# The order of the contraction tiles inside a weight block: even ones and odd ones together

## The chip, the cores and the metric

The kernel runs on one core of a Trainium2 chip. The metric is the device time of one execution in microseconds (us). The engines are TensorE (PE in the profile; its weight loads are listed apart as PEld), VectorE (DVE), ScalarE (ACT), GpSimd (POOL) and the engine that issues most transfers (SP).

## The reference

One layer of a hybrid decoder is computed for 256 positions of a new sequence and 8 × 4 positions of sequences that are under way, 288 rows of width 2048 in all, in float32:

```python
proj = x @ w_in
gB, gC, h, q, k, v, z, b_logit, a_logit, m_a, m_b = jnp.split(proj, split_points, axis=-1)
conv_out, new_conv_a = causal_depthwise_conv(gC * h, conv_a_buf, conv_a_w)
y_a = (gB * conv_out) @ w_a_out
...
o, S = gated_delta_rule(qh, kh, vh, g, beta, S0.astype(jnp.float32))
...
y_b = o.reshape(Bsz, L, D_GDN).astype(x.dtype) @ w_b_out
merged = jax.nn.sigmoid(m_a) * y_a + jax.nn.sigmoid(m_b) * y_b
x = layer_norm(ALPHA * x + merged @ w_o, ln1_g, ln1_b)
hid = jnp.square(jax.nn.relu(x @ w_up))
x = layer_norm(ALPHA * x + hid @ w_down, ln2_g, ln2_b)
```

Nearly all the work is in the products with the six large matrices: `w_in` (2048 × 11280), `w_a_out` and `w_b_out` (1024 × 2048), `w_o` (2048 × 2048), `w_up` (2048 × 8192) and `w_down` (8192 × 2048).

## The kernel before

**Products.** Activations lie transposed, the contraction on the partitions in tiles of 128, and the 288 rows along the free dimension. A product is made as out.T: the weights are the operand that is loaded into TensorE (128 × 128 at a time), the activations the one that streams past (128 × 288). To keep float32 accuracy each operand is split into a high part, rounded to a shorter format, and a low part, the rest. Three of the four products are made: high × high, high × low and low × high.

**Blocks.** The weights are read in blocks of 512 KB: 4 tiles of the contraction by 256 columns (`KB = 4`, `GW = 256`). The list `blocks`, filled by `add_group` (L154), holds all of them in the order of work. A group is a run of blocks that sum into one pair of PSUM banks, one bank for each 128 columns: 4 blocks where the contraction is 2048 long, 2 where it is 1024. There are 496 blocks: 176 of `w_in` and, between its last 64, 16 of `w_a_out` and 16 of `w_b_out`; then 32 of `w_o`; then four rounds of 32 of `w_up` and 32 of `w_down`. Blocks 0 to 47 are the groups of k, q and v. The first four blocks are wider (2 tiles by 512 columns) and serve two groups at once. The last four, marked `by_token`, are multiplied in another function with the operands exchanged.

**Stages of a block.** The main loop (L1667) goes over the block numbers `i`. SP loads the block into a `raw` tile (`load`, L191). ScalarE casts it to the high part (`split_hi`, L207, the instruction at L212); VectorE subtracts the high part from the raw block for the low part (`split_lo`, L214; it goes through the helper `tt`, so its instruction is listed at L143). From block 10 on both are done for block `i + 3` while block `i` is multiplied. A block's two parts lie in one of four buffers, `wbuf[i % 4]` (L163). Each buffer has two halves 1056 numbers (4224 bytes) apart: the even tiles of the block, high and low, are in one and the odd tiles in the other; two tiles of one half lie 256 numbers (1024 bytes) apart (`weight_halves`, L167). In a wide block a half holds one tile with its 512 columns.

**The matmuls of a block.** `matmuls(i)` (L221) goes over the tiles `k` of the block, and for each makes six matmuls. For each of the two column halves, the high weights meet the high and then the low activations (four matmuls, L245); then the low weights of each column half meet the high activations (two, L247). Every matmul has a weight load of its own. A block is 24 matmuls. `st` marks the tile whose first matmul starts a new sum in the bank, and `en` the tile whose last matmul ends it. After the last block of a group its evacuation (the functions in `gi["evac"]`) runs during the next blocks.

**What sets the order.** The program's order is written out by hand (`tc.manual_schedule()`): every engine executes its instructions in the order in which the program issues them. Waits between engines are put in from the tiles that they write and read: a matmul waits for the cast or the subtraction that wrote its weights and for the instruction that wrote its activations, and a cast into a buffer waits for the last matmul that read that buffer's high part. Between blocks the loop issues other work: the evacuations that are due, and up to the merge phase one step of the delta rule (`sgen`) for a block, with small matmuls of its own on TensorE.

Of the kernel before, what the change touches and what calls it, by code (L numbers as in the profile page):

```python
# [106 lines left out]
def hybrid_kernel(ctx: ExitStack, tc: tile.TileContext, A):  # L107
# [15 lines left out]
    def nm(s):  # L123
        counter[0] += 1
        return f"{s}{counter[0]}"
# [61 lines left out]
    def at(i, f):  # L187
        due.setdefault(i, []).append(f)
# [32 lines left out]
    def matmuls(i):  # L221
        gi, r0, k0, first, last = blocks[i]
        if gi.get("by_token"):
            return first_tokens(i, k0)
        members = gi.get("pair", (gi,))
        if first:
            for m in members:
                m["ps"] = acp.tile([P, 2, 512], F32, tag="acc", name=nm("acc"))
        ps = members[0]["ps"]
        h, l = his.pop(i), los.pop(i)  # L230
        ah, al = gi["acts"]()
        n = gi["width"]
        kb = gi["kb"]
        h, l = ([u[:, k % 2, k // 2] for k in range(KB)] if kb == KB else
                [u[:, k].rearrange("p u c -> p (u c)") for k in range(2)] for u in (h, l))
        for k in range(kb):
            xh_, xl_ = ah[:, k0 + k, 0:n], al[:, k0 + k, 0:n]
            st = first and k == 0
            en = last and k == kb - 1
            per = gi["cols"] // P // len(members)  # L240
            for u, m in enumerate(members):
                ts = [(m["ps"][:, t, 0:n], slice((per * u + t) * P, (per * u + t + 1) * P)) for t in range(per)]
                both = [(o, c, x) for o, c in ts for x in (xh_, xl_)]
                for o, c, x in both[::2] + both[1::2] if i == 0 else both:
                    pe.matmul(o, h[k][:, c], x, start=st and x is xh_, stop=False)  # L245
                for o, c in ts:
                    pe.matmul(o, l[k][:, c], xh_, start=False, stop=en)  # L247
                    if fill:
                        fill.pop(0)()
        if last:  # L250
            for n, f in enumerate(gi["evac"]):
                at(i + 1 + n, lambda f=f: f(ps))
# [514 lines left out]
    def first_tokens(i, k0):  # L767
        kept.append((his.pop(i), los.pop(i)))
        a = ph["acc"]
        if k0 == 0:  # L770
            ph["T0"] = acp.tile([P, 2, 512], F32, tag="acc", name=nm("acc"))[:, 0]
            for k in range(2):
                pe.matmul(ph["T0"][:, 256 + k * P:256 + k * P + P], a[:, 14 + k, 0:P], ident,
                          start=k == 0, stop=False, is_transpose=True)
            sample_copy(0)
            sample_copy(1)
            ph["sg2"] = gtile()
            sample_turn(2, True)
            pe.matmul(ph["sg2"][:, 256:512], cst("sel96"), ph["s4"], start=False, stop=True)
        products(ph["T0"][:, 256:512], 0, k0 // KB)  # L780
# [886 lines left out]
    for i in range(len(blocks)):  # L1667
# [72 lines left out]
        if i == mark["end"] - 1:  # L1740
            sample_products()
        matmuls(i)
        if i == 4:
            x_last()
# [47 lines left out]
```

## Time and profile before

| | us |
|---|---|
| median of 3 runs | 1642.29 (1642.19 to 1642.38) |
| the profiled execution, its own time | 1642.29 |
| its span, first to last instruction | 1640.2 |
| VectorE busy | 981.1 |
| ScalarE busy | 785.4 |
| VectorE's subtraction of 128 × 1024 at L143 (mean of 493) | 1.225 |
| ScalarE's cast of 128 × 1024 at L212 (mean of 493) | 1.048 |

How to read the profile: "busy" is the time in which an engine had an instruction under way. TensorE's matmuls overlap, so the mean duration of one (some 0.29 us) is longer than the distance between the starts of two; its pace is read from starts, or from the number of matmuls in a stretch. In a view by time a row gives the start in us from the start of the span, the duration, the engine, the line and the operands, and a row with "x2" stands for two instructions that overlap. In a view by windows a row gives the start and end of a stretch, its length, and for each engine its busy time and, in brackets, the number of instructions. The rows of waits give the waiting engine and line, what it waited for, the total, the number of times and the longest.

### The profile page before, as it was taken

To read this page: it belongs to the slowest core of one execution; us is meant where nothing else is said; L and a number is where in the kernel's file an instruction comes from. 1 tells how busy PE (TensorE), PEld (TensorE's weight loads), DVE (VectorE), ACT (ScalarE), POOL (GpSimd) and SP (SyncE) were. 2 spreads that over 40 slices of the span, in tenths; PEclk is the share of its full clock that TensorE was granted. 3 is DMA by queue.
4 is the path that set the end of the run, shared out by engine and by line. 5 is a ranking of instruction groups with operands and counts; after the bars stand their busy time and mean duration, and the time that the engine had idled before them with its cause. 6 is when DMAs were issued, how large, how long until landed. Compare 5 with 4: busy or idle time off the path is not lost.

```text
span 1640.2 us, 31402 instructions
## 1 busy us (share of the span) xinstructions
PE 1631.2 (99%) x13130; PEld 1616.4 (99%) x13130; DVE 981.1 (60%) x1299; ACT 785.4 (48%) x1231; POOL 139.0 (8%) x273
## 2 busy tenths in 40 slices
PE   9999999999999999999999999999999999999998
PEld 8999999999999999999999999999999999999998
DVE  6798688767544444457776666554444444444566
ACT  6786756448533333434444445443334433344454
POOL 1142216133000000000000000000000000000111
PEclk9999999999999999999999999999999999999999
DMA  8655457645655555555565555555555555555653
GB/s 265 184 175 168 142 174 202 182 127 171 200 167 168 168 167 168 168 168 166 166 221 159 164 169 165 169 169 168 168 167 168 168 169 168 168 167 169 182 165 102
DMA packets 273236, 280.42 MB, mean 171 GB/s; under 512 B 13727, under 2 KB 267220, under 8 KB 272832
## 3 DMA queue, kind: packets, MB, share of 16 engines
q1 hardware_dynamic: 269190, 266.06, 53.7%
q0 software_dynamic: 3616, 12.02, 2.4%
q8 instruction: 103, 1.69, 0.4%
q14 instruction: 39, 0.32, 0.1%
q10 hardware_dynamic: 288, 0.33, 0.1%
HBM read 270.88 MB, written 7.48 MB: 170 GB/s over the span
## 4 chain that ended last, share of the span: by engine, by line
PE 99%; DMA 0%; DVE 0%; ACT 0%; SPq 0%; issue 0%
PE acc L245 63%; PE acc L247 31%; PE acc L765 1%; DMA raw<-in_w_in_dram 0%; PE g L1351 0%; PE g L1523 0%; PE g L1543 0%; PE g L1546 0%; PE g L1342 0%; PE g L1243 0%; PE g L1501 0%; PE g L1535 0%; PE g L1057 0%; PE g L982 0%; PE g L719 0%; PE g L1418 0%
## 5 line engine op out<-in xcount | busy, mean ns | idle before, releaser
L143 DVE TENSOR_TENSOR w<-raw,w 128x1024 fp32r<-128x1024 f32 (+1 forms) x503 | 607.3, 1210 | 561.3 <-ACT w L212 559.6
L212 ACT CAST w<-raw 128x1024 fp32r<-128x1024 f32 (+1 forms) x499 | 518.2, 1041 | 711.3 <-PE acc L245 643.2
L245 PE MATMUL acc<-xh,w 128*128 128x288 f32 x1408 | 396.4, 298 | 0.7 <-ACT w L1625 0.4
L245 PE MATMUL acc<-xl,w 128*128 128x288 f32 x1408 | 390.8, 293 | 0.1
L247 PE MATMUL acc<-xh,w 128*128 128x288 f32 x1408 | 299.2, 293 | 0.5 <-DVE w L143 0.5
L245 PE MATMUL acc<-dh,w 128*128 128x288 f32 (+1 forms) x1024 | 287.1, 296 | 0.0
L245 PE MATMUL acc<-dl,w 128*128 128x288 f32 (+1 forms) x1024 | 285.6, 294 | 0.0
L245 PE MATMUL acc<-hh,w 128*128 128x288 f32 x992 | 276.9, 295 | 0.0
L245 PE MATMUL acc<-hl,w 128*128 128x288 f32 x992 | 275.3, 293 | 0.0
L245 PEld LDWEIGHTS acc<-xh,w 128*128 128x128 f32 x1408 | 264.4, 188 | 3.7 <-issue 1.6
L245 PEld LDWEIGHTS acc<-xl,w 128*128 128x128 f32 x1408 | 264.2, 188 | 1.2 <-DVE xl L143 0.3
L247 PEld LDWEIGHTS acc<-xh,w 128*128 128x128 f32 x1408 | 224.4, 188 | 1.0 <-DVE w L143 0.9
L247 PE MATMUL acc<-dh,w 128*128 128x288 f32 (+1 forms) x1024 | 217.3, 293 | 0.0
L247 PE MATMUL acc<-hh,w 128*128 128x288 f32 x992 | 209.6, 292 | 0.0
L245 PEld LDWEIGHTS acc<-dh,w 128*128 128x128 f32 x1024 | 192.4, 188 | 0.0
L245 PEld LDWEIGHTS acc<-dl,w 128*128 128x128 f32 x1024 | 192.3, 188 | 0.0
L245 PEld LDWEIGHTS acc<-hh,w 128*128 128x128 f32 x992 | 186.4, 188 | 0.4 <-issue 0.4
L245 PEld LDWEIGHTS acc<-hl,w 128*128 128x128 f32 x992 | 186.2, 188 | 0.0
L247 PEld LDWEIGHTS acc<-dh,w 128*128 128x128 f32 x1024 | 163.4, 188 | 0.0
L247 PEld LDWEIGHTS acc<-hh,w 128*128 128x128 f32 x992 | 157.7, 188 | 0.0
L245 PE MATMUL acc<-mh,w 128*128 128x288 f32 x256 | 71.4, 295 | 0.0
L245 PE MATMUL acc<-ml,w 128*128 128x288 f32 x256 | 71.0, 293 | 0.0
(420 smaller groups left out, 1477.3 us busy)
## 6 DMA issues: line engine op xcount, KB each, us to landing
raw<-in_w_in_dram SPq DMA_DIRECT2D x175, 512.0 KB, 3.8
raw<-in_w_up_dram SPq DMA_DIRECT2D x128, 512.0 KB, 3.6
raw<-in_w_down_dram SPq DMA_DIRECT2D x128, 512.0 KB, 3.6
raw<-in_w_o_dram SPq DMA_DIRECT2D x32, 512.0 KB, 4.3
raw<-in_w_a_out_dram SPq DMA_DIRECT2D x16, 512.0 KB, 3.6
raw<-in_w_b_out_dram SPq DMA_DIRECT2D x16, 512.0 KB, 3.6
S<-in_state_gdn_dram POOLq DMA_DIRECT2D x8, 512.0 KB, 5.1
out_dram<-S POOLq DMA_DIRECT2D x8, 512.0 KB, 4.1
```

The lines of the kernel that those rows point to most:

```text
L143: dve.tensor_tensor(out=out, in0=a, in1=b, op=op)
L212: act.copy(his[i][:, a, b], r[:, a, b])
L245: pe.matmul(o, h[k][:, c], x, start=st and x is xh_, stop=False)
L247: pe.matmul(o, l[k][:, c], xh_, start=False, stop=en)
L765: pe.matmul(out, x[:, kk, c], w[:, k % 2, k // 2], start=False, stop=stop)
```

## The change

In the inner loop of `matmuls`, the tiles of a block are no longer taken as 0, 1, 2, 3. From block 10 on, odd-numbered blocks take 0, 2, 1, 3 and even-numbered ones 1, 3, 0, 2. The marks for the start and the end of a sum go with the first and the last tile of the new order. Blocks 0 to 9 keep the old order, and the last four blocks, which leave `matmuls` earlier, are not touched. The number of matmuls and their operands are the same.

```diff
@@ -233,10 +233,11 @@
         kb = gi["kb"]
         h, l = ([u[:, k % 2, k // 2] for k in range(KB)] if kb == KB else
                 [u[:, k].rearrange("p u c -> p (u c)") for k in range(2)] for u in (h, l))
-        for k in range(kb):
+        ks = ((0, 2, 1, 3) if i % 2 else (1, 3, 0, 2)) if i > 9 else range(kb)
+        for k in ks:
             xh_, xl_ = ah[:, k0 + k, 0:n], al[:, k0 + k, 0:n]
-            st = first and k == 0
-            en = last and k == kb - 1
+            st = first and k == ks[0]
+            en = last and k == ks[-1]
             per = gi["cols"] // P // len(members)
             for u, m in enumerate(members):
```

## The prediction

> **What bounds the kernel now.** I looked first at the clock and the span, then at the share of each engine, then at the chain that ended last, then at TensorE's own waits.
>
> ```profile
> span 1640.2 us, 31402 instructions
> PE 1631.2 (99%) x13130; PEld 1616.4 (99%) x13130; DVE 981.1 (60%) x1299; ACT 785.4 (48%) x1231; POOL 139.0 (8%) x273
> ...
> PE 99%; DMA 0%; DVE 0%; ACT 0%; SPq 0%; issue 0%
> PE acc L245 63%; PE acc L247 31%; PE acc L765 1%; DMA raw<-in_w_in_dram 0%; PE g L1351 0%; PE g L1523 0%; PE g L1543 0%; PE g L1546 0%; PE g L1342 0%; PE g L1243 0%; PE g L1501 0%; PE g L1535 0%; PE g L1057 0%; PE g L982 0%; PE g L719 0%; PE g L1418 0%
> ...
> PE acc L247 <- DVE w L143: 0.5, 1, 0.5
> PE acc L245 <- ACT w L1625: 0.4, 1, 0.4
> ```
>
> TensorE is busy for 99% of the span, and 94% of the chain are the two lines that the change reorders, L245 and L247. These matmuls wait for another engine only in single cases of half a microsecond. So the time is the number of matmuls times their pace; nothing else matters unless it makes TensorE wait. The pace comes from a view by windows:
>
> ```profile
> core 0: us, PE busy (x) PEld busy (x) DVE busy (x) ACT busy (x) POOL busy (x), PEclk, DMA share, GB/s
> 430.00:710.00 280.00, 280.00 (x2138) 280.00 (x2137) 132.14 (x120) 109.22 (x115) 0.00 (x0) 1.00 0.58 167
> 1330.00:1610.00 280.00, 280.00 (x2138) 280.00 (x2137) 142.13 (x151) 112.07 (x138) 9.33 (x27) 1.00 0.56 170
> ```
>
> Both stretches hold 2138 matmuls in 280 us at full granted clock (PEclk 1.00): 280 / 2138 = 131 ns each. The reader should see what differs between them: other activation tiles at other places, another matrix, 10 us more of VectorE work, GpSimd at work in one only. The count is the same to one in 2138, or 0.05%. The pace thus comes from the kind and order of the instructions (each with its own weight load), not from what the other engines write meanwhile.
>
> **The change part by part.**
>
> *Instructions.* None is added or removed. Each tile of the contraction still takes six matmuls of the same shapes, and a block its 24; the number of weight loads, casts, subtractions and transfers stays as it is. This part costs 0.
>
> *How many blocks.* The change acts from block 10 on and not in the last four blocks, which take another path.
>
> ```profile
> raw<-in_w_in_dram SPq DMA_DIRECT2D x175, 512.0 KB, 3.8
> raw<-in_w_up_dram SPq DMA_DIRECT2D x128, 512.0 KB, 3.6
> raw<-in_w_down_dram SPq DMA_DIRECT2D x128, 512.0 KB, 3.6
> raw<-in_w_o_dram SPq DMA_DIRECT2D x32, 512.0 KB, 4.3
> raw<-in_w_a_out_dram SPq DMA_DIRECT2D x16, 512.0 KB, 3.6
> raw<-in_w_b_out_dram SPq DMA_DIRECT2D x16, 512.0 KB, 3.6
> ```
>
> One such transfer brings one block: 495, and with the first block, which comes in pieces, 496. Less 10 and less 4 leaves 482 blocks. The even tiles of a block lie in one half of its weight buffer and the odd ones in the other. The old order 0, 1, 2, 3 changes the half at each of four tile changes (the one into the next block included). The new order (0, 2, 1, 3 in odd blocks; 1, 3, 0, 2 in even ones) changes it only in the middle of a block, because a block starts in the half in which the last one ended. So 3 × 482 = 1446 tile changes that now cross from one half to the other will stay in one half.
>
> *What a tile change inside one half costs.* From block 10 on the trace of before has none, but block 2 does. There the columns are twice as wide, one half holds one tile with all 512 columns, and the twelve matmuls of a tile go to two groups, six and six. A step from the first six to the second stays in the half, and makes the same jump in the buffer as a step from tile 0 to 2 or 1 to 3 does in the new order. Starts, in the view by time:
>
> ```profile
> 15.58 0.30 PE L245 MATMUL acc<-xh,w 128*128 128x288 f32 x1
> ...
> 17.15 0.29 PE L245 MATMUL acc<-xh,w 128*128 128x288 f32 x1
> ...
> 17.94 0.29 PE L245 MATMUL acc<-xh,w 128*128 128x288 f32 x1
> ...
> 18.73 0.30 PE L245 MATMUL acc<-xh,w 128*128 128x288 f32 x1
> ```
>
> The six that end with a step inside the half (17.15 to 17.94) take 0.79 us, and the six that end with a crossing (17.94 to 18.73) take 0.79 us as well. The whole of block 2, with two crossings, takes 18.73 - 15.58 = 3.15 us. An ordinary block with four:
>
> ```profile
> 22.89 0.30 PE L245 MATMUL acc<-xh,w 128*128 128x288 f32 x1
> ...
> 26.03 0.30 PE L245 MATMUL acc<-xh,w 128*128 128x288 f32 x1
> ```
>
> takes 3.14 us. Two crossings less made no difference beyond the 0.01 us to which the view gives a start. I take 0 ns for a tile change inside a half against one that crosses; the ends that the resolution leaves are 0.01 us over two crossings, 5 ns either way. Another reason for 0: five of the six loads of any tile already follow a load from the same half, so the new order brings no new kind of neighbour. What block 2 can't show is the other operand, whose tile stays there and changes by two in the new order; but the matmuls of a tile already take turns between two activation tiles that lie much farther apart. Sum: 1446 × 0 = 0, with ends at 1446 × 5 ns = 7.2 us either way.
>
> *The release of a weight buffer.* ScalarE may cast block i+3 into a buffer when the last matmul with the high parts of block i-1 has read it; VectorE then fills the low parts.
>
> ```profile
> ACT w L212 <- PE acc L245: 643.2, 344, 4.0
> ...
> 999.25 1.05 ACT L212 CAST w<-raw 128x1024 fp32r<-128x1024 f32 x1 [0.25 <-PE acc L245]
> ...
> 1000.33 1.23 DVE L143 TENSOR_TENSOR w<-raw,w 128x1024 fp32r<-128x1024 f32 x1 [1.49 <-ACT w L212]
> ```
>
> The last matmul of that kind is the 22nd of its block, whichever tile comes last, so the cast starts when it does now. Even a shift of a whole tile, 0.79 us, would be covered: the low parts are ready at 1000.33 + 1.23 = 1001.56, and their block starts three blocks after 999.3, at about 1008.7, 7 us later. The queues of ScalarE, VectorE, SP and POOL keep their order, and no wait is added in any. Cost 0. Without that cover it would be as in this place of the chain in order of time, where a subtraction came late and the one wait of 0.5 us above arose:
>
> ```profile
> 122.05 1.23 DVE w L143
> ```
>
> *A tile taken earlier than now.* The third or fourth tile of a block may now come second or first, and its activations must be there by then. The tightest place is a last pair of tiles that the preceding group has just produced.
>
> ```profile
> 1130.48 0.75 DVE L143 TENSOR_TENSOR hl<-r,hh 128x576 fp32r<-128x576 f32 x1
> ...
> 1134.62 0.29 PE L245 MATMUL acc<-hh,w 128*128 128x288 f32 x1
> ```
>
> This pair is complete at 1130.48 + 0.75 = 1131.23, and the block that reads it starts at 1134.62. Even read first in its block it would have been there for 3.4 us. Cost 0. The first matmul of a group (which starts the accumulation) and the last keep their places, so the evacuation of each sum starts as before.
>
> **Sum.** 0 + 0 + 0 + 0 on a profiled execution of 1642.29 us (span 1640.2, some 2 us around it), which is also the median of the runs shown (1642.29, from 1642.19 to 1642.38). I predict **1642.3 us**. Two kernels count as different here from 0.2% on, 3.3 us.
>
> **The rivals.**
>
> *A, slower: a jump inside a half delays TensorE.* Two tiles of one half lie 1024 bytes apart; a load right behind one from the same half but another tile could take longer. The pace does depend on the form of the operands:
>
> ```profile
> 825.00:915.00 90.00, 90.00 (x669) 90.00 (x668) 60.62 (x72) 42.46 (x62) 0.00 (x0) 1.00 0.57 182
> 925.00:1015.00 90.00, 90.00 (x688) 90.00 (x688) 63.17 (x76) 46.46 (x60) 0.00 (x0) 1.00 0.55 167
> ```
>
> With 290 columns in place of 288 (the first row) a matmul takes 90 / 669 = 134.5 ns against 90 / 688 = 130.8: two columns of 288 should bring 0.9 ns and brought 3.7. If each jump cost that, 1446 × 3.7 = 5.4 us: 1647.7. It counts from 3.3 / 1446 = 2.3 ns per jump. Against it stands block 2. Chance 0.04.
>
> *B, faster: it is the crossing that costs today.* Then 1446 of them go. At the end that the resolution leaves, 5 ns each, that is 7.2 us: 1635.1. For it: a matmul takes 131 ns, and no row says which part of that is needed. Against it: the six matmuls with a crossing and the six without one in block 2 take the same. Chance 0.05.
> On B, the Trainium skill ("TensorE: Matmul & The Clock Gate", section "Back-to-back issue gap") gives an isolated warm matmul N / 2.4 + 2.5 ns, 122.5 ns for 288 columns as an estimate; the trace's 131 ns is 8.5 ns above that, and were this excess at a crossing due to the crossing, the sum would be 1446 × 8.5 ns = 12.3 us, 1630.0. But the trace shows the excess as a mean over all matmuls, five of six of which have no crossing.
> The same skill ("SBUF — State Buffer", section "Who interferes with whom") says that TensorE has one read port for weights and another for the moving operand and waits for nobody; by this rule A and B both come to 0, and the trace's equal counts in the two windows of 280 us agree.
>
> *C, slower: a new wait for the split.* If a release or a first use came in the wrong place, the groups of q, k and v, where the late subtraction stood, would feel it: they are the blocks up to 47, 38 of them from block 10 on, and at the price of the one wait there, 0.5 us each, 19 us: 1661. It counts from 3.3 / 38 = 0.09 us a block. Against it stands that both come at the same turn as now. Chance 0.01.
>
> *No effect, because the order does not reach the chip.* The program's order of matmuls is written out by hand and goes to TensorE as it stands, so I give this no chance of its own; its time would be that of the forecast.
>
> **How the numbers follow.** Forecast 0.90, A 0.04, B 0.05, C 0.01. That gives faster 0.05, same 0.90, slower 0.05. The forecast alone holds more than 8 in 10, so the range is its own. How far an unchanged pace repeats, the two windows of 280 us show: one matmul in 2138, 0.05%, or 0.8 us of 1640; with the 0.1 us by which the runs lie apart that is 0.9 either way, 1641.4 to 1643.2. The ends at 5 ns a jump lie in A and B, outside.
>
> **What would show it.** In the profile after, the windows 430 to 710 and 1330 to 1610 should again hold 2138 matmuls, give or take two; a jump cost of 2.3 ns would show as about 5 fewer, since 280 us hold 89 blocks with three jumps each (0.6 us, 5 matmuls); B would show as more. ScalarE's cast should still be released by L245, about 344 times, and L245 and L247 should still wait some 0.9 us in all. I am wrong if the tile changes in the view by time no longer lie 0.78 to 0.79 us apart, or if L245 or L247 begins to wait for ScalarE or VectorE.

## The result, and the profile after

| | before | after |
|---|---|---|
| median of 7 runs, us | 1642.38 (1641.32 to 1643.58) | 1648.41 (1646.53 to 1648.68) |
| the profiled execution, us | 1642.29 | 1646.96 |
| its span, us | 1640.2 | 1645.1 |

The changed kernel takes 1.0033 of the time before, with a 95% interval from 1.0021 to 1.0044: it is slower, by 5.4 us by this ratio and by 6.0 by the medians, outside the predicted range. The seven times of the changed kernel fall into two groups, 1646.5 to 1647.0 and 1648.4 to 1648.7; what parts them isn't known, and the profiled execution belongs to the first.

The page of the changed kernel has the same picture as before: one engine, two lines.

```profile
span 1645.1 us, 31359 instructions
...
PE 1637.1 (100%) x13130; PEld 1622.4 (99%) x13130; DVE 981.4 (60%) x1299; ACT 784.4 (48%) x1231; POOL 137.4 (8%) x273
```

TensorE's waits in the changed kernel (what waited, for what, us in total, times, longest):

```profile
PE acc L248 <- DVE w L143: 0.4, 1, 0.4
...
PE acc L246 <- ACT xh L972: 0.2, 1, 0.2
```

The lines have moved down by one (L245 and L247 are now L246 and L248). TensorE still has 13130 matmuls, and its waits on these two lines come to 0.6 us. Still it is busy for 5.9 us longer, 1637.1 against 1631.2 us. So no wait was added and no work: the pace has changed. The view by windows shows it, and shows where:

```profile
core 0: us, PE busy (x) PEld busy (x) DVE busy (x) ACT busy (x) POOL busy (x), PEclk, DMA share, GB/s
430.00:710.00 280.00, 280.00 (x2129) 280.00 (x2128) 132.21 (x120) 108.54 (x114) 0.00 (x0) 1.00 0.57 167
1330.00:1610.00 280.00, 280.00 (x2129) 280.00 (x2128) 140.29 (x148) 112.44 (x136) 9.32 (x27) 1.00 0.55 169
825.00:915.00 90.00, 90.00 (x669) 90.00 (x668) 60.78 (x73) 41.99 (x60) 0.00 (x0) 1.00 0.58 186
```

Both stretches of 280 us hold 2129 matmuls where they held 2138, at full granted clock. 9 matmuls of 131 ns over the 89 blocks of such a stretch are 13.2 ns a block. In the third row, the blocks with 290 columns, the count is 669 as before: there the order costs nothing. Of the 482 blocks that the change touches, 32 are of that kind; 450 × 13.2 ns = 5.9 us, about the 6.0 us by which the medians differ. (The two profiled executions differ by 4.7 us. The changed one was ahead by some 0.6 us before block 10, where the code is the same, and up to the end of the delta rule other small matmuls come between the blocks.)

At the edges of blocks the chain in order of time, for the changed kernel, shows the four matmuls of L246 and the two of L248 in turn:

```profile
1330.21 0.26 PE acc L248 x2
1330.47 0.54 PE acc L246 x4
1331.01 0.26 PE acc L248 x2
1331.28 0.52 PE acc L246 x4
...
1333.37 0.27 PE acc L248 x2
1333.63 0.54 PE acc L246 x4
1334.17 0.26 PE acc L248 x2
1334.43 0.52 PE acc L246 x4
```

Each row starts where the one before it ends. The first tile of a block takes 1331.28 - 1330.47 = 0.81 us in one block and 1334.43 - 1333.63 = 0.80 us in the next; the usual tile had 0.78 to 0.79. So the loss sits around the edges of blocks. The starts of the matmuls in the kept traces, averaged over the blocks that lie whole in the two stretches, say it more sharply: a block takes 3160.0 ns against 3146.7 before, 13.3 more. Against run 1 below, which has the block time of before, the last matmul of a block takes 3.4 ns longer and the first four of the next together 10.1 ns.

One more thing moved, and turned out to cost nothing: the cast now waits in half of the blocks for the other line.

```profile
ACT w L212 <- PE acc L248: 375.3, 178, 3.0
ACT w L212 <- PE acc L246: 283.4, 169, 3.8
```

Before, all 344 such waits were for the high-weight line. The layout of a buffer offers a reason, argued and not tested by itself: the low parts of the first half lie between the high parts of the two halves, inside the stretch that the cast's view spans, while the low parts of the second half lie behind it. Runs 5 and 6 agree with it: where every block ends in the first half all these waits are for the low-weight line, and where every block ends in the second all are for the high-weight line. So a cast waits for more than the last reader of the high part, which is what the description of the kernel says.

### The profile page after: what moved, and what is told of

It reads as the page before. It is cut to its first block, busy times and chain, and to the rows that moved or that the text cites. A ratio compares the mean times of both kernels' runs of the same rounds, so it can differ in the third digit from the quotient of the medians.

```text
span 1645.1 us, 31359 instructions
## 1 busy us (share of the span) xinstructions
PE 1637.1 (100%) x13130; PEld 1622.4 (99%) x13130; DVE 981.4 (60%) x1299; ACT 784.4 (48%) x1231; POOL 137.4 (8%) x273
## 4 chain that ended last, share of the span: by engine, by line
PE 98%; DVE 1%; ACT 1%; DMA 0%; issue 0%; SPq 0%; ACTq 0%
PE acc L246 62%; PE acc L248 31%; PE acc L766 1%; PE g L1352 0%; PE g L1524 0%; PE g L1544 0%; PE g L1547 0%; DMA xr<-in_x_prompt_dram 0%; PE g L1343 0%; PE g L1244 0%; PE g L1502 0%; DVE w L143 0%; PE g L1536 0%; DVE w L146 0%; ACT w L212 0%
## 5 line engine op out<-in xcount | busy, mean ns | idle before, releaser
L246 PE MATMUL acc<-xh,w 128*128 128x288 f32 x1408 | 396.4, 298 | 0.3 <-ACT xh L972 0.2
L246 PE MATMUL acc<-xl,w 128*128 128x288 f32 x1408 | 392.6, 294 | 0.0
L248 PE MATMUL acc<-xh,w 128*128 128x288 f32 x1408 | 300.6, 294 | 0.4 <-DVE w L143 0.4
L246 PE MATMUL acc<-dl,w 128*128 128x288 f32 (+1 forms) x1024 | 286.8, 295 | 0.0
L246 PE MATMUL acc<-dh,w 128*128 128x288 f32 (+1 forms) x1024 | 286.7, 295 | 0.0
L246 PE MATMUL acc<-hl,w 128*128 128x288 f32 x992 | 276.8, 294 | 0.0
L246 PE MATMUL acc<-hh,w 128*128 128x288 f32 x992 | 276.7, 295 | 0.0
L246 PEld LDWEIGHTS acc<-xh,w 128*128 128x128 f32 x1408 | 264.7, 188 | 3.1 <-issue 1.6
L246 PEld LDWEIGHTS acc<-xl,w 128*128 128x128 f32 x1408 | 264.8, 188 | 1.0
L248 PEld LDWEIGHTS acc<-xh,w 128*128 128x128 f32 x1408 | 226.3, 189 | 0.8 <-DVE w L143 0.8
L248 PE MATMUL acc<-dh,w 128*128 128x288 f32 (+1 forms) x1024 | 218.2, 294 | 0.0
L248 PE MATMUL acc<-hh,w 128*128 128x288 f32 x992 | 210.6, 293 | 0.0
L246 PEld LDWEIGHTS acc<-dl,w 128*128 128x128 f32 x1024 | 192.4, 188 | 0.0
L246 PEld LDWEIGHTS acc<-dh,w 128*128 128x128 f32 x1024 | 192.4, 188 | 0.0
L246 PEld LDWEIGHTS acc<-hh,w 128*128 128x128 f32 x992 | 186.3, 188 | 0.4 <-issue 0.4
L246 PEld LDWEIGHTS acc<-hl,w 128*128 128x128 f32 x992 | 186.5, 188 | 0.0
L248 PEld LDWEIGHTS acc<-dh,w 128*128 128x128 f32 x1024 | 164.7, 188 | 0.0
L248 PEld LDWEIGHTS acc<-hh,w 128*128 128x128 f32 x992 | 159.4, 189 | 0.0
L246 PE MATMUL acc<-ml,w 128*128 128x288 f32 x256 | 71.5, 294 | 0.0
L246 PE MATMUL acc<-mh,w 128*128 128x288 f32 x256 | 71.4, 295 | 0.0
```

## The experiments

All experiments are read by one measure that is finer than the time: how many matmuls start in the stretches 430 to 710 us and 1330 to 1610 us. A matmul more or less in 2138 is 0.05%. The order of the weights is written as the halves of the buffer that the tiles lie in: 0 for the first half, 1 for the second. Four theories went in: (1) each jump inside a half costs; (2) the new order of the activation tiles costs; (3) the edge of two blocks inside one half costs; (4) the later release of the buffer costs. The diffs show the lines that differ from the changed kernel, and in runs 8, 10 and 12 from the kernel before.

**1. Without the turn in every second block** (halves 0 0 1 1 in every block).

```diff
-        ks = ((0, 2, 1, 3) if i % 2 else (1, 3, 0, 2)) if i > 9 else range(kb)
+        ks = ((0, 2, 1, 3)) if i > 9 else range(kb)
```

> All blocks from 10 on take the tiles 0, 2, 1, 3; the turn in every second block is left out. Inside a block two tile changes stay in a half of the buffer, as with the change; at the edge of two blocks the half changes, as before. The measure is the number of matmuls that start in the stretches 430 to 710 and 1330 to 1610 us (2138 before, 2129 with the change: 13.4 ns a block over 89 blocks). Theory 1, each jump inside a half costs (13.4 / 3 = 4.5 ns): 2 jumps a block, 8.9 ns, 2132 matmuls, about +4.3 us. Theory 2, the new order of the activation tiles costs: 2129, or near it, +6 us. Theory 3, only the edge costs, where one block ends and the next starts in the same half: 2138, +0 us. Theory 4, only the later release costs, in blocks that end in the first half: 2138, +0 us.

```profile
430.00:710.00 280.00, 280.00 (x2138) 280.00 (x2137) 132.13 (x120) 109.31 (x114) 0.00 (x0) 1.00 0.54 168
1330.00:1610.00 280.00, 280.00 (x2137) 280.00 (x2137) 141.67 (x150) 111.84 (x135) 9.33 (x27) 1.00 0.55 170
```

The pace of before is back, with two jumps inside a half in every block and the activation tiles in the new order. The first two theories fall: neither the jumps nor that order costs by itself. (The time was 1644.03 against 1641.88 us, ratio 1.0010, interval 1.0001 to 1.0019. The pace in the two stretches doesn't show that; in the profiled execution 0.9 of its 1.8 us more are there at block 10, before the first block that the edit reaches, and another 0.5 come between blocks 200 and 240.)

**2. Halves only**: the natural order of the tiles, with tiles 0 and 1 in the first half and 2 and 3 in the second.

```diff
-        return t.rearrange("p (u r) c -> p r u c" if blocks[i][0]["kb"] == KB else "p (r u) c -> p r u c", r=2)
+        pairs = i > 9 and not blocks[i][0].get("by_token")
+        return t.rearrange("p (u r) c -> p r u c" if blocks[i][0]["kb"] == KB and not pairs else "p (r u) c -> p r u c", r=2)
...
-        h, l = ([u[:, k % 2, k // 2] for k in range(KB)] if kb == KB else
+        h, l = ([u[:, k // 2, k % 2] if i > 9 else u[:, k % 2, k // 2] for k in range(KB)] if kb == KB else
...
-        ks = ((0, 2, 1, 3) if i % 2 else (1, 3, 0, 2)) if i > 9 else range(kb)
+        ks = ((0, 1, 2, 3)) if i > 9 else range(kb)
```

> Natural order 0, 1, 2, 3 in all blocks, but from block 10 on tiles 0 and 1 lie in the first half of the buffer and 2 and 3 in the second. The weights are read half by half as in the first run, the activations in their old order. Theory 1 (jumps inside a half): 2 a block, 2132 matmuls in each stretch of 280 us, +4.3 us. Theory 2 (order of the activation tiles): 2138, +0 us. Theories 3 and 4 (edge, release): 2138, +0 us.

```profile
430.00:710.00 280.00, 280.00 (x2122) 280.00 (x2121) 130.73 (x120) 108.05 (x113) 0.00 (x0) 1.00 0.55 168
```

Slower than the change: 16 matmuls fewer than before, 23.6 ns a block; time 1651.27 us, ratio 1.0052 (1.0035 to 1.0069). No theory had said so. The halves run 0 0 1 1 as in the first run, and there it was free; what differs is which activation tile meets which half.

**3. Tiles only**: the order of the change on the placing of run 2, so that the halves run 0 1 0 1 in every block.

> The order of the change (0, 2, 1, 3 and 1, 3, 0, 2) on the placing of the second run, so that the weights change the half at every tile, as before, while the activation tiles are taken as in the change. Theory 1: no jump inside a half, 2138 matmuls in 280 us, +0 us. Theory 2: the whole cost, 2129, +6 us. Theories 3 and 4: every block starts in the first half and ends in the second, 2138, +0 us.

```profile
430.00:710.00 280.00, 280.00 (x2127) 280.00 (x2126) 131.34 (x120) 108.00 (x113) 0.00 (x0) 1.00 0.54 168
```

11 matmuls fewer; time 1650.38 us, ratio 1.0046 (1.0031 to 1.0061). Taken alone this would have spoken for theory 2, which run 1 had just refuted. Runs 2 and 3 have in common that even activation tiles no longer always go with one half and odd ones with the other. That gave a new theory, "place": the start of the weights against the start of the activation tile, modulo 256 bytes, sets the pace. The rows of the activation tiles are 1152 or 1408 bytes long and the halves 4224 bytes apart, all three odd multiples of 128. Call the start of a tile modulo 256 bytes its foot. In the layout of the built program the activations of these products begin on a multiple of 256, and the weights in all four buffers 112 bytes past one. So in the kernel before, even tiles of both operands stand on one foot and odd ones 128 bytes off it, together.

**4. The edge only** (halves 0 1 0 1, then 1 0 1 0).

```diff
-        ks = ((0, 2, 1, 3) if i % 2 else (1, 3, 0, 2)) if i > 9 else range(kb)
+        ks = ((0, 1, 2, 3) if i % 2 else (1, 0, 3, 2)) if i > 9 else range(kb)
```

> Odd blocks take 0, 1, 2, 3, even ones 1, 0, 3, 2: inside a block the half changes at every tile, only at the edge of two blocks it stays. Theory 1: 1 jump a block, 4.5 ns, 2135 matmuls in 280 us, +2.1 us. Theory 2: the activation tiles are in another new order, somewhere between 2129 and 2138. Theories 3 and 4: the whole cost, 2129, +6 us.

```profile
430.00:710.00 280.00, 280.00 (x2124) 280.00 (x2124) 131.03 (x120) 108.58 (x114) 0.00 (x0) 1.00 0.54 167
1330.00:1610.00 280.00, 280.00 (x2124) 280.00 (x2123) 139.02 (x146) 112.40 (x136) 9.33 (x27) 1.00 0.55 169
```

14 matmuls fewer, 20.6 ns a block; time 1650.39 us, ratio 1.0047 (1.0032 to 1.0062). The theory of the edge and that of the release both still stood, and a third had joined them, "count": the change has one change of half per block, this run three, and both are slow; before has four and run 1 two, and both are fast. With an odd number the next block starts in the other half than this one, and its tiles on the other foot. The next four runs set these against each other and against "place".

**5. Every block ends in the first half** (halves 1 1 0 0 in every block).

```diff
-        ks = ((0, 2, 1, 3) if i % 2 else (1, 3, 0, 2)) if i > 9 else range(kb)
+        ks = ((1, 3, 0, 2)) if i > 9 else range(kb)
```

> All blocks from 10 on take 1, 3, 0, 2: every block ends in the first half of its buffer, every next one starts in the second, so the half changes at the edge and once inside. The measure is again the number of matmuls in the stretches 430 to 710 and 1330 to 1610 us (2138 before, 2129 with the change, 2138 without the turn, 2124 with the edge alone). Theory release (a block that ends in the first half sets its buffer free 0.26 us later and this costs): at least the whole cost, 2129 or fewer. Theory edge (an edge of two blocks inside one half costs): 2138. Theory count (what costs is an odd number of half changes per block, which makes every second block start on the other foot; the change has 1, the edge alone 3, before 4, without the turn 2): two changes, 2138. Theory place (the place of a weight tile modulo 256 bytes against that of the activation tile, which the second and the third run broke, costs): kept here, 2138.

```profile
430.00:710.00 280.00, 280.00 (x2138) 280.00 (x2137) 132.20 (x120) 108.97 (x115) 0.00 (x0) 1.00 0.55 168
1330.00:1610.00 280.00, 280.00 (x2138) 280.00 (x2137) 141.68 (x151) 111.94 (x136) 9.33 (x27) 1.00 0.56 170
```

The waits of this kernel show that here the release is the late one all the time:

```profile
ACT w L212 <- PE acc L248: 647.8, 348, 4.0
```

All 348 waits are for the last line, and the pace is that of before (one run, 1642.37 against 1642.84 us). The release is not the cause.

**6. Every edge inside a half** (halves 1 0 0 1 in every block).

```diff
-        ks = ((0, 2, 1, 3) if i % 2 else (1, 3, 0, 2)) if i > 9 else range(kb)
+        ks = ((1, 0, 2, 3)) if i > 9 else range(kb)
```

> All blocks from 10 on take 1, 0, 2, 3: every block starts and ends in the second half, so the half stays at the edge of two blocks and changes twice inside. The buffers come free as early as before. Theory release: 2138. Theory edge: every edge stays in its half, 2129 to 2124. Theory count: two changes a block, 2138. Theory place: 2138.

```profile
430.00:710.00 280.00, 280.00 (x2137) 280.00 (x2137) 132.17 (x120) 108.92 (x115) 0.00 (x0) 1.00 0.55 168
1330.00:1610.00 280.00, 280.00 (x2138) 280.00 (x2137) 142.19 (x151) 112.16 (x138) 9.32 (x27) 1.00 0.56 170
```

Free (one run, 1642.33 us), though every edge of two blocks stays in its half. The theory of the edge falls.

**7. Three changes of half, and every edge crosses** (halves 0 1 1 0, then 1 0 0 1).

```diff
-        ks = ((0, 2, 1, 3) if i % 2 else (1, 3, 0, 2)) if i > 9 else range(kb)
+        ks = ((0, 1, 3, 2) if i % 2 else (1, 0, 2, 3)) if i > 9 else range(kb)
```

> Odd blocks take 0, 1, 3, 2, even ones 1, 0, 2, 3: three half changes a block, one step inside a half in the middle of the block, and every edge of two blocks changes the half. Theory release: odd blocks end in the first half, half of the blocks, about 2129 to 2138. Theory edge: 2138. Theory count: three changes, odd, 2124 as in the run with the edge alone. Theory place: 2138.

```profile
430.00:710.00 280.00, 280.00 (x2125) 280.00 (x2124) 130.75 (x120) 107.94 (x113) 0.00 (x0) 1.00 0.55 168
1330.00:1610.00 280.00, 280.00 (x2124) 280.00 (x2123) 139.28 (x146) 111.71 (x136) 9.33 (x27) 1.00 0.55 168
```

As slow as run 4 (one run, 1651.29 us), with the one step inside a half in the middle of the block and not at its edge. Only "count" had said 2124. The starts in the traces show that the loss doesn't belong to the edge as such: a tile of before takes 786.7 ns on average, and the slowest one, 795.4 ns in both runs, is the tile right behind the step inside a half, in run 4 the first of a block and in run 7 the third.

**8. Halves exchanged** (natural order; halves 1 0 1 0, even tiles now in the second half).

```diff
+        if swapped(i):
+            return [(k, slice(None)) for k in range(2)]
...
-                act.copy(his[i][:, a, b], r[:, a, b])
+                act.copy(his[i][:, place(i, a), b], r[:, a, b])
```

Here `swapped(i)` holds from block 10 to the last four, and `place` gives the other half; the subtraction and the list of weight tiles go the same way.

> Natural order 0, 1, 2, 3 in all blocks, but from block 10 on the even tiles lie in the second half of the buffer and the odd ones in the first (the cast and the subtraction are made in two instructions of half the size each, which lengthens ScalarE's and VectorE's work by some 0.2 us a block). The half changes at every tile as before; only the place of weights against activations modulo 256 bytes is the other way round (even activation tiles start at a multiple of 256 bytes, odd ones 128 bytes past it; the first half starts 112 bytes past one, the second 240). Theory place: a cost, 2129 or fewer. Theories edge and count: 2138. Theory release: every block ends in the first half, 2129 or fewer.

```profile
430.00:710.00 280.00, 280.00 (x2111) 280.00 (x2110) 142.98 (x206) 123.98 (x201) 0.00 (x0) 1.00 0.55 167
1330.00:1610.00 280.00, 280.00 (x2111) 280.00 (x2110) 151.26 (x231) 127.25 (x221) 9.11 (x27) 1.00 0.55 168
```

27 matmuls fewer, 39.7 ns a block (one run, 1656.14 us). The order and the number of changes are as before the change, and every block starts in the same half as the one before it. The theory of the release doesn't apply: with the cast made in two parts, its waits are for the line of the high weights, L253 in this kernel:

```profile
ACT w L220 <- PE acc L253: 594.6, 723, 3.7
```

The longer work of ScalarE and VectorE shows in their columns (124 and 143 us of 280) and leaves them far from full. What is left is the place of one operand against the other, or the split into two parts, which run 12 doesn't have and loses as much. (At 39.7 ns in each of 450 blocks the time would be 17.9 us longer, and it is 13.3. By the starts in the trace, blocks 48 to 100, with small matmuls between them, lose 0.3 us and not 2.1, and the 32 blocks with 290 columns gain 0.4.)

**9. The turn after every second block.**

```diff
-        ks = ((0, 2, 1, 3) if i % 2 else (1, 3, 0, 2)) if i > 9 else range(kb)
+        ks = ((0, 2, 1, 3) if i % 4 < 2 else (1, 3, 0, 2)) if i > 9 else range(kb)
```

> The change with the turn after every second block: two blocks take 0, 2, 1, 3, the next two 1, 3, 0, 2, and so on. Every block changes the half once inside, and every second edge of two blocks changes it too, so odd and even counts take turns. Measure: matmuls in the stretches 430 to 710 and 1330 to 1610 us. Theory count per block (each block edge that stays in a half puts the next block on the other foot, and that costs 13.4 ns each time): half as many such edges, 6.7 ns a block on average, 2133 or 2134, about +3 us. Rival, only the count over a whole period matters (six changes in four blocks, even): 2138; the same rule would have made the change itself free, so it is weak. Rival, a turn brings a lasting slower state: 2129 or fewer.

```profile
430.00:710.00 280.00, 280.00 (x2133) 280.00 (x2133) 132.18 (x120) 109.21 (x114) 0.00 (x0) 1.00 0.55 168
1330.00:1610.00 280.00, 280.00 (x2134) 280.00 (x2132) 141.76 (x149) 112.54 (x137) 9.36 (x27) 1.00 0.56 170
```

Half of the loss, as "count" had it (one run, 1645.29 us): every second block starts on the other foot than its predecessor, and the loss is that of one such start for every two blocks. It is no lasting slower state.

**10 and 11. No shift between the halves** (4096 bytes apart in place of 4224), with the order of before and with that of the change.

```diff
-            views.append(bass.AP(t.tensor, t.offset, [t.ap[0], (1056, 2), (256, 2), (1, 256)]))
+            views.append(bass.AP(t.tensor, t.offset, [t.ap[0], (1024, 2), (256, 2), (1, 256)]))
```

> The kernel before, natural order, with the second half of each weight buffer 4096 bytes behind the first in place of 4224, so that both halves start 112 bytes past a multiple of 256. Even tiles keep their place against the activations, odd ones get the one that all tiles had in the run with the halves swapped. Theory place (the start of the weights against that of the activations modulo 256 bytes sets the pace): between before (2138) and the swapped run (2111), near 2124, about +9 us. Rival, being in the one or the other half is what counts: 2138. Rival, the release of the buffers: unchanged here, 2138.

> The changed kernel with the halves 4096 bytes apart. As many tiles as in the run before this one stand in the worse place. Theory place alone: near 2124 matmuls in 280 us, as there. Theory count, if the other foot comes from the activation tiles: fewer than that run by up to 9. If it comes from the weights alone, which no longer shift: the same as that run.

The old order:

```profile
430.00:710.00 280.00, 280.00 (x2120) 280.00 (x2119) 130.68 (x119) 108.36 (x114) 0.00 (x0) 1.00 0.55 167
1330.00:1610.00 280.00, 280.00 (x2133) 280.00 (x2132) 140.90 (x148) 112.14 (x136) 9.36 (x27) 1.00 0.55 169
```

The new order:

```profile
430.00:710.00 280.00, 280.00 (x2122) 280.00 (x2121) 130.97 (x119) 108.71 (x114) 0.00 (x0) 1.00 0.55 167
1330.00:1610.00 280.00, 280.00 (x2121) 280.00 (x2120) 139.07 (x146) 111.72 (x136) 9.36 (x27) 1.00 0.55 168
```

Removing the 128 bytes alone slows the old order (one run, 1648.08 us), so it is the address that counts and not the half as such. But its two stretches differ, 2120 and 2133, with one and the same order: with mixed places the pace depends on something more than place and order, perhaps on what went before; no run shows on what. (It isn't the addresses of the activations: in the blocks of `w_down`, in the second stretch, they lie where x lay in the first, and such a block takes 3153 ns where one that reads x takes 3173.) For this reason the pair doesn't tell whether the other foot comes from the weights or from the activations; that question got no answer (the new order: one run, 1651.26 us).

**12. The weights 16 bytes further on.**

```diff
-        wbuf.append(wp.tile([P, 4 + 2 * 1024 + 32], F32R, tag=f"w{u}", name=f"w{u}", bufs=1))
+        wbuf.append(wp.tile([P, 8 + 2 * 1024 + 32], F32R, tag=f"w{u}", name=f"w{u}", bufs=1))
...
-        for o in (4, 516):
+        for o in (8, 520):
```

> The kernel before with the weights 16 bytes further on in their buffers (8 numbers of padding in place of 4): they start 128 or 0 bytes past a multiple of 256, in place of 112 or 240. Theory place, if only steps of 128 bytes matter: 2138. If the 16 bytes matter too: fewer matmuls in 280 us, down to 2111, or more.

```profile
430.00:710.00 280.00, 280.00 (x2111) 280.00 (x2110) 129.32 (x117) 107.33 (x112) 0.00 (x0) 1.00 0.55 168
1330.00:1610.00 280.00, 280.00 (x2111) 280.00 (x2111) 136.64 (x142) 110.67 (x133) 9.32 (x27) 1.00 0.54 166
```

Four numbers of padding more, and the kernel before loses 39.7 ns a block (one run, 1660.35 us); no other tile of the built program lies elsewhere than before. The edit moves the weights against the activations and against the multiples of 128 bytes at once, so it doesn't tell which of the two costs.

The runs that keep the placing of before, side by side. "Starts elsewhere" says how many blocks start in the other half than the block before them; the counts are those of the two stretches.

| order | halves | changes a block | starts elsewhere | matmuls in 280 us |
|---|---|---|---|---|
| before | 0 1 0 1 | 4 | none | 2138, 2138 |
| without the turn (1) | 0 0 1 1 | 2 | none | 2138, 2137 |
| ends first (5) | 1 1 0 0 | 2 | none | 2138, 2138 |
| every edge inside (6) | 1 0 0 1 | 2 | none | 2137, 2138 |
| turn after two (9) | 0 0 1 1 twice, 1 1 0 0 twice | 2 and 1 | half | 2133, 2134 |
| the change | 0 0 1 1, 1 1 0 0 | 1 | all | 2129, 2129 |
| edge only (4) | 0 1 0 1, 1 0 1 0 | 3 | all | 2124, 2124 |
| three changes (7) | 0 1 1 0, 1 0 0 1 | 3 | all | 2125, 2124 |

Written as one endless row of halves, these eight orders are only five sequences. Runs 1, 5 and 6 are the same one begun at another place, two tiles of each half in turn, and their blocks take the same 3146.7 ns. Runs 4 and 7 are the same one too: two tiles of a half, one, one, and again (3166.7 ns both). The change has four tiles of each half in turn, run 9 four, two and two. So "a block that starts in the other half pays" is one way to put what the slow sequences have in common. Another is that four tiles of one half in a row cost 13.3 ns, and a pair among single tiles 20.0. No run separates the two. Blocks with halves 0 1 0 1 and 0 0 1 1 in turn would: every one starts in the first half, and pairs stand among single tiles.

## Why the prediction was wrong

**What bounds the kernel: right.** The time is the number of matmuls times their pace, before and after. The reading that went with it, that the pace comes from kind and order alone because two stretches with other tiles had equal counts, was wrong. Those tiles differ in place, but all of them step by odd multiples of 128 bytes, so the two stretches were alike in the one respect that counts. Runs 8 and 12 move the weights by 128 and by 16 bytes and lose 27 matmuls.

**No instruction added: right**, 13130 matmuls in both. **482 blocks: right**, but 32 of them, with 290 columns, don't feel the change.

**"What a tile change inside one half costs" is the step that failed.** It put 1446 jumps at 0 ns each. The jump is indeed free: run 1 has two in each block and keeps the pace. The error was to see the change as 1446 separate jumps and add them. What costs shows only in the sequence over several blocks: with the change each block starts in the other half than the one before, and each such start comes with a loss of 13.2 ns. Block 2, the evidence for the step, has the halves 0 0 1 1, which is the sequence of run 1 and free. It tested the jump and was silent on the sequence. The sign that the prediction named for being wrong, tile changes no longer 0.78 to 0.79 us apart, showed with 0.81 and 0.80.

**The release: wrong in half of the blocks, without effect.** The cast was said to wait for the 22nd matmul, whichever tile comes last. After a block that ends in the first half it waits for the last line instead (178 of 347 waits), against the prediction's sign of about 344 waits for the high-weight line. The cover that the prediction named, 7 us, holds: run 5 has the late release everywhere and the time of before.

**A tile taken earlier: right.** TensorE waits for nothing new: 0.6 us on its two lines. (The prediction's 0.9 us for before left out a row of 0.2.)

**The rivals.** A gave 1647.7 us, close to the measured 1648.41, and that is luck: its mechanism, a price for every jump inside a half, is refuted by runs 1 and 6. B went the wrong way; C fell, since TensorE's waits didn't grow. The passages from the Trainium skill weighed the same two ideas, a gain at the crossings and no dependence on place; the runs bear out neither. The Trainium skill ("SBUF — State Buffer", section "Who interferes with whom") has TensorE read its two operands through independent ports and wait for nobody. Here 16 bytes of padding changed TensorE's pace by 1.3%, 2138 to 2111 matmuls, and no run shows by what means.

**What stays open** is why. That the weights' start against the activations' modulo 256 bytes sets the pace, and that a block which starts on the other foot pays once, are rules that fit the runs and not a shown mechanism; no view shows what makes them. Neither rule is complete: run 10 has two paces with one placing and one order, and the second rule can't be told from that of the pairs and rows of four above. Whether the weights or the activations carry the foot wasn't separated, and why three changes cost 20.6 ns where one costs 13.2 isn't known.

## What to carry to other kernels

Where TensorE's pace is the time, the addresses of its two operands are part of the schedule: count the matmuls in equal stretches before and after any edit of order or padding, since a shift of 0.4% shows there to one in two thousand. A comparison inside the old trace only tests what differs in it; before it is used as a bound, ask what its two sides have in common. And an order that brings every block back to where it began is the one to try first: with the placing of before, the two sequences here that did so were free, and the three that didn't were slower.

## What the runs showed of the hardware

- The padding of a weight buffer changed the pace of back-to-back matmuls: weights that start 112 bytes past a multiple of 256 against activations that start on it gave 2138 matmuls in 280 us; 128 bytes past, 2111 (run 12); exchanged by 128 bytes, 2111 (run 8).
- The same order ran at two paces in one kernel, 2120 and 2133 (run 10).
- The blocks with 290 columns follow another rule. In the changed kernel their count is that of before, 669 in 90 us, and the placing of run 2, which is slow everywhere else, is the faster one there, as the stretch 835 to 915 us shows, first before, then run 2:

```profile
835.00:915.00 80.00, 80.00 (x594) 80.00 (x594) 53.35 (x62) 36.55 (x54) 0.00 (x0) 1.00 0.56 173
```

```profile
835.00:915.00 80.00, 80.00 (x599) 80.00 (x599) 54.21 (x63) 38.26 (x54) 0.00 (x0) 1.00 0.56 172
```

594 matmuls against 599, 0.8% for these 32 blocks. The placing of run 8 has 597 there, that of run 12 has 593.
